# Out-projection of a hybrid decoder trunk: six pairs of heads by seven products in place of five, four plain heads in place of six, and the last part by blocks of tokens

## The chip, the cores and the metric

The kernel runs on one core of one Trainium2 chip. The metric is device time in microseconds (us). The core has TensorE (PE: matmuls, with weight loads in a row of their own, PEld), VectorE (DVE), ScalarE (ACT), GpSimd (POOL) and SyncE (SP), which here only issues transfers. Each works through its own list of instructions in order, and waits where one needs a result that another has not finished.

## The reference

One decoder layer on 512 tokens and 16 learned tokens ahead of them, all float32: RMS norm, one input projection, three token mixers on separate heads (6 gated DeltaNet heads, 5 gated linear attention heads, 5 heads of softmax attention with a forgetting gate), each head 128 wide and multiplied by its own SiLU gate, one output projection of the 16 heads, a residual add and a last RMS norm.

```python
def hybrid_layer(x, norm_w, w_in, ..., w_out):
    h = rms_norm(x, norm_w)
    proj = (h @ w_in).astype(f32)
    ...
    o = jnp.concatenate([o_dn, o_gla, o_fox], axis=-1)[:, PAD:].astype(x.dtype)
    return x + o @ w_out            # o: 512 x 2048, w_out: 2048 x 2048

def reference(...):
    ...
    return rms_norm(h, final_norm_w)[:, N_META:]
```

## The kernel before, in words

**Arithmetic.** Every large matmul is made of three: a float32 operand is split into a high part (rounded to the PE's float32r, an ACT cast) and a low part (the rest, a DVE subtraction), and hi·hi, hi·lo and lo·hi are added up in PSUM. A weight tile is 128 x 1024; `split` (L167 the cast, L168 the subtraction) makes the two parts of each. The raw tiles come through two buffers; every third weight of the products takes three buffers from the pool `six` instead, which also holds the attention heads' keys and queries (`fqk`), the loaded head outputs and the residual.

**Stages.** Until about 792 us the input projection and the three mixers run, interleaved, the last of them attention head 4. The output projection follows, on tiles of 128 tokens by 512 columns (`mms`, L1401: one call is three matmuls). It has two ways:

- *Products.* The first `SH` = 10 heads are taken in pairs. With a pair as a 2 x 2 of blocks (head by half of the tokens) and the weights as a 2 x 2 too, seven products of sums take the place of eight, as in Strassen's scheme in Winograd's form. Each product is 12 matmuls of 512 columns per pair. The operands are a11, a12, s2, s1, s3, s4, a22, in this order of products; the sums of heads that they need are DVE rows of 128 x 256 (L627 and L628 the first sums, L1447 and L1478 the differences), and each operand is split in its turn (L1379 cast, L613 subtraction, 128 x 256 each). The sums of weights for the products are made earlier, as small "chores" that move tiles to scratch memory and add them there by transfers.
- *Plain heads.* The other six heads go by ordinary matmuls. An *early part* (PSUM tiles `pa`) does four of them for column banks 0 to 2, ahead of the products. The *last part* (`pt`, `pz`) does the remaining two heads for banks 0 to 2, then bank 3 with all six heads, with the last block of tokens cut in two halves of 256 columns.

**What sets the order.** A scheduler in the build gives each engine one list; the program fixes parts of it by hand: `paced` rows follow each other on ACT and DVE, `high_priority` puts the splits and the early part's adds forward, and attention head 4's matmuls are placed by number among the early ones. Head 4 goes by four blocks of queries: per block scores (`pfa` L1228, `pfd` L1229), their maximum and weights (DVE L1232 and L1234, ACT L1238, DVE L1239 to L1243), transposes (`pfx` L1246, split by ACT L1250 and DVE L1251), and at the end the product with the values (`pfo` L1276 to L1279).

**After a tile.** `add` (L1420, DVE) adds a PSUM tile to the residual, which `begin` (L1395) has loaded; `square` (L1427, ACT) sums squares for the last norm, `weigh` (L1430, GpSimd) multiplies by the norm's weight, and L1604 to L1614 scale and store.

## Time and profile before

| | |
|---|---|
| median of three runs | 972.87 us (972.32 to 974.4) |
| the profiled execution's own time | 972.28 us |
| its span in the profile | 970.6 us |
| granted TensorE clock, mean | 0.997 |
| PE busy | 960.8 us (99%) |
| DVE busy | 673.0 us (69%) |
| ACT busy | 476.4 us (49%) |
| POOL busy | 221.2 us (23%) |

How to read it: a row of a group gives line, engine, operation, tiles (out<-in), shape and count, then busy time in us, the mean of one in ns, and the engine's idle time before with what ended it. A row of the chain of waits gives start, duration and the work that set the end, followed back from the last instruction. A row of stretches gives from:to and length, then for PE, PEld, DVE, ACT and POOL the busy us and instructions, then the granted clock, the share of the 16 transfer engines that is busy, and GB/s. A timeline row gives start, duration, engine, line and tiles; where it stands for several (x5) the duration is that of all. Next to each other on one engine, rows can overlap by their fill: the pitch is the distance of two starts.

### The profile page before, as it was taken

The page shows a single profiled execution, that of the slowest core. Times are in us where ns is not written, and L with a number is a line of the kernel's source. Part 1 is how long each engine was busy: PE and PEld are TensorE (multiplying, and loading weights), DVE is VectorE, ACT ScalarE, POOL GpSimd, SP SyncE. Part 2 cuts the span into 40 slices and gives each one's busy share as a digit, 9 for nine tenths or more (in the row PEclk, how much of TensorE's full clock was granted, in tenths as well). Part 3 has the DMA queues.
Part 4 walks back from the last instruction along what each step waited for, and adds up shares of the span by engine and source line. Part 5 has one row for each costly group of instructions (what it writes and reads, how often), then busy time and mean ns, then how long its engine had stood idle before and what let it go on. Part 6 is the DMA issues. An engine that isn't in the chain of part 4 may idle for free.

```text
span 970.6 us, 18917 instructions
## 1 busy us (share of the span) xinstructions
PE 960.8 (99%) x7301; PEld 885.2 (91%) x7301; DVE 673.0 (69%) x1463; ACT 476.4 (49%) x1046; POOL 221.2 (23%) x243
## 2 busy tenths in 40 slices
PE   9999999999999999999999999999999999999996
PEld 7899999899999878899999989899999998888885
DVE  6467767877658886434685957867867768977664
ACT  7754433345356233334545545555555545644345
POOL 0032322232123225111213223223332120000033
PEclk9999999999999999999999999999999999999998
DMA  9736677988558687734647575688775587366535
GB/s 353 297 135 208 195 195 213 283 230 224 176 151 232 208 237 196 192 106 104 166 129 189 147 195 172 182 227 210 205 207 163 177 288 273 131 209 222 182 126 174
DMA packets 70336, 191.87 MB, mean 198 GB/s; under 512 B 14078, under 2 KB 17326, under 8 KB 69477
## 3 DMA queue, kind: packets, MB, share of 16 engines
q1 hardware_dynamic: 46048, 152.64, 45.4%
q0 software_dynamic: 15104, 31.66, 18.2%
q10 hardware_dynamic: 9092, 6.36, 2.4%
q8 instruction: 57, 0.93, 0.4%
q14 instruction: 35, 0.28, 0.1%
HBM read 179.94 MB, written 60.88 MB: 248 GB/s over the span
## 4 chain that ended last, share of the span: by engine, by line
PE 98%; DVE 1%; issue 0%; DMA 0%; ACT 0%; SPq 0%; DVEq 0%
PE pp L235 49%; PE pp_a L560 8%; PE pq L1401 6%; PE pp L314 5%; PE pa L1401 3%; PE pt L1401 3%; PE ps L1401 3%; PE pp_c L560 2%; PE pp_d L560 2%; PE pp_b L560 2%; PE pr L1401 1%; PE pss L1046 1%; PE pfo L1276 1%; PE pgate L408 1%; PE pfa L1228 1%; PE pg L704 1%
## 5 line engine op out<-in xcount | busy, mean ns | idle before, releaser
L235 PE MATMUL pp<-xh,wlo 128*128 128x264 f32 (+2 forms) x1120 | 270.0, 305 | 0.0
L235 PE MATMUL pp<-xl,whi 128*128 128x264 f32 (+2 forms) x1120 | 269.6, 305 | 0.0
L235 PE MATMUL pp<-xh,whi 128*128 128x264 f32 (+2 forms) x1120 | 269.5, 305 | 0.0
L167 ACT CAST whi<-raw 128x1024 fp32r<-128x1024 f32 x131 | 137.2, 1047 | 179.5 <-PE pp L235 110.1
L168 DVE TENSOR_TENSOR wlo<-raw,whi 128x1024 fp32r<-128x1024 f32 x131 | 160.6, 1226 | 59.5 <-ACT whi L167 50.1
L235 PEld LDWEIGHTS pp<-xh,wlo 128*128 128x128 f32 x1120 | 181.5, 189 | 9.2 <-DVE wlo L168 0.7
L235 PEld LDWEIGHTS pp<-xh,whi 128*128 128x128 f32 x1120 | 181.3, 188 | 8.7 <-issue 0.2
L235 PEld LDWEIGHTS pp<-xl,whi 128*128 128x128 f32 x1120 | 181.6, 189 | 8.2
L367 POOL TENSOR_SCALAR stc<-cv 128x528 f32<-128x528 f32 (+1 forms) x18 | 27.2, 1513 | 132.0 <-DVE cv L602 120.9
L602 DVE SCALAR_TENSOR_TENSOR cv<-pb,cpk,cv 128x528 f32<-128x528 f32 (+1 forms) x54 | 40.9, 757 | 0.8
L1430 POOL TENSOR_TENSOR acc<-acc,fw 128x512 f32<-128x512 f32 x4 | 6.1, 1544 | 138.4 <-DVE wll L168 138.4
L168 DVE TENSOR_TENSOR wlos<-raws,whis 128x1024 fp32r<-128x1024 f32 x20 | 24.3, 1223 | 15.0 <-ACT whis L167 15.0
L167 ACT CAST whis<-raws 128x1024 fp32r<-128x1024 f32 x20 | 20.7, 1050 | 28.2 <-PE ps L1401 9.2
L314 PE MATMUL pp<-xh,wf 128*128 128x512 f32 x128 | 33.1, 398 | 0.3 <-ACT wf L291 0.3
L314 PEld LDWEIGHTS pp<-xh,wf 128*128 128x128 f32 x128 | 24.2, 190 | 6.1 <-ACT wf L291 0.6
L560 PE MATMUL pp_a<-t,whi 128*128 128x264 f32 (+1 forms) x224 | 29.4, 282 | 0.0
L356 DVE TENSOR_TENSOR pb<-pp,rstd 128x264 f32<-128x264 f32 (+1 forms) x36 | 13.8, 425 | 22.1 <-PE pp L235 22.0
L560 PE MATMUL pp_a<-xl,whi 128*128 128x264 f32 x112 | 28.4, 288 | 0.0
L560 PE MATMUL pp_a<-xh,whi 128*128 128x264 f32 x112 | 28.1, 285 | 0.0
L560 PEld LDWEIGHTS pp_a<-t,whi 128*128 128x128 f32 x224 | 27.6, 188 | 0.0
L474 POOL DMA_DIRECT2D tw<-tw x16 | 13.4, 837 | 60.9 <-DVE wlo L168 29.5
L1401 PE MATMUL pq<-whia,a 128*128 128x512 f32 x80 | 25.5, 394 | 0.0
(487 smaller groups left out, 2058.2 us busy)
## 6 DMA issues: line engine op xcount, KB each, us to landing
raw<-in_w_in SPq DMA_DIRECT2D x103, 512.0 KB, 3.9
ti<-in_w_in SPq DMA_DIRECT2D x28, 512.0 KB, 5.4
raw<-ti SPq DMA_DIRECT2D x28, 512.0 KB, 3.4
tw<-in_w_dn SPq DMA_DIRECT2D x20, 512.0 KB, 5.3
raws<-tw SPq DMA_DIRECT2D x15, 512.0 KB, 3.7
ti<-in_w_in POOLq DMA_DIRECT2D x14, 512.0 KB, 7.0
ti<-ti POOLq DMA_DIRECT2D x14, 512.0 KB, 6.7
tw<-in_w_dn POOLq DMA_DIRECT2D x10, 512.0 KB, 6.7
```

The source lines that it names most:

```text
L167: pace[0] = A.copy(hi, raw).ins
L168: pace[1] = V.tensor_tensor(out=lo, in0=raw, in1=hi.bitcast(F32), op=ALU.subtract).ins
L235: mm = PE.matmul(p_[:, :nt], wt[:, j * m : (j + 1) * m], xx[k][:, t0 : t0 + nt], start=(k == 0 and wt is hi and xx is xh), stop=(k == KT - ...
L314: PE.matmul(begun[i][0][0][:, :S], wt[:, i * P : (i + 1) * P], xx[k][:, NM:T], start=k + n == 0, stop=k == KT - 1 and n == 2)
L356: V.tensor_tensor(out=o, in0=p_[rows], in1=rstd[rows, t0 : t0 + n], op=ALU.mult)
L367: maxes.append(G.tensor_scalar_max(t, src, LOW).ins)
L408: PE.matmul(pgate[a][:, :HT], wg[k // 8][:, k % 8, :], xx[k][:, a * HT : (a + 1) * HT], start=(k == 0 and xx is xh), stop=(k == KT - 1 and ...
L474: x = G.dma_start(out=out_[s], in_=in_[s], accum_op=ALU.add, max_dma_last_dim=2048)
L560: m = PE.matmul(p_[:, cols], wt[:, j * P : (j + 1) * P], xx[j][part_][:, cols], start=first and i == 0, stop=i == len(todo) - 1, skip_grou ...
L602: V.scalar_tensor_tensor(out=c, in0=pb[:, t0 + w : w + T], scalar=cwc[:, blk, w : w + 1], in1=c, op0=ALU.mult, op1=ALU.add)
L704: PE.matmul(pg[:r, j * r : (j + 1) * r], kT[:, j, ts], kT[:, j, ts], start=True, stop=True)
L1401: mm = PE.matmul(p_, o_[:, s], w_, start=(first and n == 0), stop=(last and n == 2), skip_group_check=True)
```

## The change

Four edits.

1. `SH` is 12: six pairs go by products, four heads stay plain. Of these, two are in the early part, so it has one weight of 1024 columns per bank in place of two, and 72 matmuls in place of 144; the products have 504 in place of 420.
2. The operand steps that stood between the early part's six weights now follow its three: all head loads (`load_zr`) go out ahead of the early part, the sums and operands behind each bank.
3. The first sums (two per pair, twelve) are GpSimd's (`G.tensor_tensor`), and are not paced.
4. The last part: two banks in place of three are done for all tokens; bank 2 is done together with bank 3, block of tokens by block, with its add, square and product by the norm's weight in between. Bank 3 has four plain heads in place of six. The chores have a sixth pair of sums of weights.

Behind line 149 the new program's numbers are one higher, from line 610 on one lower: the split is L168 and L169, `mms` L1400, the add L1419, the operand's subtraction L612, the first sums L626 and L627, the differences L1450 and L1476, the attention rows L1227 to L1278.

```diff
-SH = 10
+SH = 12
...
-            paced(V.tensor_tensor(out=r["s1"], in0=r["a22"], in1=r["a21"], op=ALU.subtract),
-                  V.tensor_tensor(out=r["s3"], in0=r["a11"], in1=r["a21"], op=ALU.subtract))
+            G.tensor_tensor(out=r["s1"], in0=r["a22"], in1=r["a21"], op=ALU.subtract)
+            G.tensor_tensor(out=r["s3"], in0=r["a11"], in1=r["a21"], op=ALU.subtract)
...
-    AHEAD = {(0, -1): (0.55, (-1, -2, -3, -4, -5, -6, -7), (0, 1, 2, 3, 4)), ("f", 1): (0.26,)}
+    AHEAD = {(0, -1): (0.55, (-1, -2, -3, -4, -5, -6, -7), (0, 1, 2, 3, 4, 5)), ("f", 1): (0.26,)}
...
-    EARLY, LAST = NP - 2, NP - 6
+    EARLY = NP - 2
...
+    def columns(cc, a, b):
+        src = w_out[cc, a // 2][:, a % 2 * 512 : a % 2 * 512 + (b - a) * 512]
+        return halves(load_half(src, f"o{cc}_{a}"))
+
+    def run(pa, cc, a, b, first, last):
+        w = columns(cc, a, b)
+        for i in range(a, b):
             for tb in range(4):
-                mms(pa[tb], oparts[2 * kp + j], w[j], slice(tb * P, (tb + 1) * P), first and j == 0, last and j == 1)
+                mms(pa[tb], oparts[i], w[i - a], slice(tb * P, (tb + 1) * P), first and i == a, last and i == b - 1)
...
-    steps = [lambda a=a: rest(a, min(a + 2, EARLY)) for a in range(2, EARLY, 2)] + [load_zr]
-    steps += [quarters, lambda: operand("a11"), lambda: operand("a12")]
-    rest(0, 2)
+    steps = [quarters, lambda: operand("a11"), lambda: operand("a12")]
+    rest(0, EARLY)
+    load_zr()
     head["pa", 0] = len(order)
     for cc in range(3):
         pa = banks(psb, f"pa{cc}")
-        for kp in range(EARLY // 2):
-            run(pa, cc, kp, kp == 0, kp == EARLY // 2 - 1)
-            if kp == 1:
-                for tb in range(4):
-                    begin(tb, cc)
-            if steps:
-                steps.pop(0)()
+        run(pa, cc, 0, EARLY, True, True)
+        for tb in range(4):
+            begin(tb, cc)
+        steps.pop(0)()
         with tc.high_priority(offset=1000000):
             for tb in range(4):
                 last = add(tb, cc, pa[tb])
-    for f in steps:
-        f()
     pace[1] = last.ins
     first_sums()
     differences()
...
+    for cc in range(2):
+        pa = banks(psb if cc else psm, f"pt{cc}")
+        run(pa, cc, EARLY, NP, True, True)
+        load_last(cc)
...
+    w2 = columns(2, EARLY, NP)
+    pa, pc = banks(psm, "pt3"), banks(psb, "pt2")
     scaled = []
     for tb in range(4):
         cuts = 2 if tb == 3 else 1
+        for i in range(EARLY, NP):
+            mms(pc[tb], oparts[i], w2[i - EARLY], slice(tb * P, (tb + 1) * P), i == EARLY, i == NP - 1)
+        x = add(tb, 2, pc[tb]).ins
...
+        square(tb, 2)
+        weigh(tb, 2)
```

How it moves instructions, at three places. First DVE before, from the end of attention head 4's block 3 (`fp_9752`, weights of the block) to the second product split; `pa_9990` to `pa_9993` are the early part's last tiles, `wloa` is the low part of a product's weight:

```order
L1243 TENSOR_SCALAR fp_9752<-fp_9752,fsm_9753 128x512
L1241 SCALAR_TENSOR_TENSOR fm_9664<-fp_9752,fsm_9753,fm_9664 128x16
L168 TENSOR_TENSOR wloa_10199<-rawa_10196,whia_10198 128x1024
L1420 TENSOR_TENSOR accs_9969<-accs_9969,pa_9990 128x512
L1420 TENSOR_TENSOR accs_9969<-accs_9969,pa_9991 128x512
L1420 TENSOR_TENSOR accs_10071<-accs_10071,pa_9992 128x512
L1251 TENSOR_TENSOR fplo_9666<-pfx_9762,fphi_9665 128x3x128
L1420 TENSOR_TENSOR accs_10071<-accs_10071,pa_9993 128x512
...
L168 TENSOR_TENSOR wloa_10217<-rawa_10214,whia_10216 128x1024
```

And DVE now, from the adds of the early part's last two tiles to the first product split:

```order
L1419 TENSOR_TENSOR accs_9973<-accs_9973,pa_9939 128x512
L1419 TENSOR_TENSOR accs_9973<-accs_9973,pa_9940 128x512
L1450 SCALAR_TENSOR_TENSOR zr_9811<-zr_9811 128x256
...
L1450 SCALAR_TENSOR_TENSOR zr_9826<-zr_9826 128x256
L1250 TENSOR_TENSOR fplo_9675<-pfx_9710,fphi_9674 128x2x128
L1476 SCALAR_TENSOR_TENSOR zr_9811<-zr_9811 128x256
L1171 TENSOR_TENSOR vlo_9723<-pvf_9717,vhi_9722 128x384
L1231 ISA fp_9741,fsm_9742<-pfa_9737,fqk_9064 128x272
...
L1176 TENSOR_TENSOR fm_9673<-pwf_9727,fm_9673 128x128
L1476 SCALAR_TENSOR_TENSOR zr_9814<-zr_9814 128x256
L612 TENSOR_TENSOR s_0_10016<-zr_9811,s_0_10016 128x256
...
L169 TENSOR_TENSOR wloa_10138<-rawa_10135,whia_10137 128x1024
```

Of the rows left out, the first four are L1450; the others, behind `s_0`, are L1476 and L612 by turns (two more L612) with L1476 last. The first product split now stands behind all adds of the early part, behind the differences of all pairs and behind the first half of operand s2; before, it stood ahead of the last bank's adds.

PE before, where head 4's block 3 has its scores (`pfa_9748`, `pfd_9749`); 34 early matmuls follow there up to the transposes `pfx_9762`:

```order
L1246 MATMUL pfx_9742<-ident,fp_9732 128x128 x3
L1228 MATMUL pfa_9748<-fqk_9059 128x400
L1229 MATMUL pfd_9749<-fqk_9059 128x128
L1401 MATMUL pa_9990<-whio_1_10041,oh_9836 128x512
L1401 MATMUL pa_9991<-whio_1_10041,oh_9836 128x512
```

PE now, from the last early matmul over the scores of block 2 to the first matmul that reads the first product's low part:

```order
L1400 MATMUL pa_9940<-whio_0_9943,ol_9808 128x512
L1245 MATMUL pfx_9710<-ident,fp_9700 128x128 x2
L1168 MATMUL pvf_9717<-ident,vf_9066 128x128 x4
L1174 MATMUL pwf_9727<-ident,fs_9715 128x128
L1227 MATMUL pfa_9737<-fqk_9064 128x272
L1228 MATMUL pfd_9738<-fqk_9064 128x128
L1400 MATMUL pq_10127<-whia_10137,a_0_9915 128x512
...
L1400 MATMUL pq_10130<-whia_10137,a_0_9915 128x512
L1400 MATMUL pq_10127<-wloa_10138,a_0_9915 128x512
```

And from the second product weight's last matmul over block 3 to the use of its weights:

```order
L1400 MATMUL pq_10130<-whia_10155,a_1_9918 128x512
L1245 MATMUL pfx_9751<-ident,fp_9741 128x128 x3
L1227 MATMUL pfa_9757<-fqk_9064 128x400
L1228 MATMUL pfd_9758<-fqk_9064 128x128
L1400 MATMUL pq_10127<-whia_10173,a_2_9921 128x512
...
L1400 MATMUL pq_10130<-whia_10173,a_2_9921 128x512
L1245 MATMUL pfx_9771<-ident,fp_9761 128x128 x4
L1267 MATMUL pfw_9781<-ident,fm_9673 128x128
L1275 MATMUL pfo_9787<-fphi_9674,vhi_9722 128x512
...
L1278 MATMUL pfo_9787<-ptm_9779,fm_9673 128x512 x2
L1400 MATMUL pq_10127<-wloa_10174,a_2_9921 128x512
```

The rows left out are four-tile runs of the same weight and more `pfo`. Blocks 2 and 3 of head 4 now stand behind the early part, among the first three weights of the first product.

More of the change, by code (lines that the diff above doesn't have):

```diff
@@ L151, in load_half @@
         lo = wp.tile([P, 1024], F32R, tag="lo", name=f"wlo{name}")
+        raw, hi, lo = (t[:, : src.shape[-1]] for t in (raw, hi, lo))
         split(raw, hi, lo)
@@ L1402, in mms @@
             order.append(mm.ins)
-    halves = lambda w: [[t[:, j * 512 : (j + 1) * 512] for t in w] for j in range(2)]
+    halves = lambda w: [[t[:, j * 512 : (j + 1) * 512] for t in w] for j in range(w[0].shape[-1] // 512)]
     def load_last(kp):
@@ L1430, in weigh @@
         return G.tensor_tensor(out=acc[tb, cc], in0=acc[tb, cc], in1=fw[cc], op=ALU.mult)
-    def run(pa, cc, kp, first, last):
-        w = halves(load_half(w_out[cc, kp], f"o{cc}_{kp}"))
-        for j in range(2):
+    def columns(cc, a, b):
[4 more added lines that the diff above has]
+        for i in range(a, b):
             for tb in range(4):
-                mms(pa[tb], oparts[2 * kp + j], w[j], slice(tb * P, (tb + 1) * P), first and j == 0, last and j == 1)
+                mms(pa[tb], oparts[i], w[i - a], slice(tb * P, (tb + 1) * P), first and i == a, last and i == b - 1)
     def banks(where, name):
@@ L1553, in tile_hybrid_trunk @@
         fw.append(f)
-    for cc in range(4):
-        pa = banks(psb if cc % 2 else psm, f"pt{cc}")
-        kps = [(NP // 2 - 1,)] * 3 + [range(NP // 2)] * (3 - 3) + [range(LAST // 2)]
-        kps = kps[cc]
-        for kp in kps:
-            run(pa, cc, kp, kp == kps[0], kp == kps[-1])
-            if cc < 3 and (3 == 3 or cc == 2 and kp >= NP // 2 - 3):
-                load_last(kp if cc == 2 and 3 < 3 else NP // 2 - 3 + cc)
-                marks.append(splits[-1])
-        if cc == 3:
-            break
+    for cc in range(2):
+        pa = banks(psb if cc else psm, f"pt{cc}")
+        run(pa, cc, EARLY, NP, True, True)
+        load_last(cc)
+        marks.append(splits[-1])
         for tb in range(4):
```

25 lines of the change are left out of this document (12 added, 13 removed).

## The prediction, on record before the result was known

> **What bounds the kernel now.** I read the page's busy times and chain first, then a table of stretches, then the chain of waits from 792 us on, where the edited code runs.
>
> ```profile
> span 970.6 us, 18917 instructions
> PE 960.8 (99%) x7301; PEld 885.2 (91%) x7301; DVE 673.0 (69%) x1463; ACT 476.4 (49%) x1046; POOL 221.2 (23%) x243
> PE 98%; DVE 1%; issue 0%; DMA 0%; ACT 0%; SPq 0%; DVEq 0%
> ...
> 792.00:829.00 37.00, 36.96 (x172) 29.93 (x172) 27.12 (x71) 15.50 (x34) 4.36 (x4) 1.00 0.80 283
> 829.00:860.00 31.00, 31.00 (x140) 25.39 (x139) 29.81 (x56) 18.77 (x34) 0.00 (x0) 1.00 0.46 158
> 960.00:971.00 11.00, 2.63 (x23) 2.42 (x21) 4.23 (x13) 3.88 (x10) 0.00 (x0) 0.73 0.71 247
> ```
>
> PE is the bound: 98% of the chain, and full in the stretches that the change rewrites. So any matmul taken away is worth its pitch, and any microsecond in which PE waits is a microsecond of the program. The second thing to see is how near VectorE (DVE, third pair of numbers) comes: 27.1 of 37 us while the early part and fox head 4 run, then 29.8 of 31. The early part now is a cover: while PE works it off, the other engines do fox head 4's softmax and prepare the products.
>
> ```profile
> 804.06 0.22 PE pfx L1246 x2
> 804.28 0.44 PE pvf L1169 x4
> 804.72 0.11 PE pwf L1175
> 804.83 0.46 PE pfa L1228 x2
> ...
> 819.99 0.67 PE pfa L1228 x2
> 820.66 0.22 PE pfd L1229 x2
> 820.88 7.85 PE pa L1401 x34
> 828.74 0.44 PE pfx L1246 x4
> 829.17 0.11 PE pfw L1268
> 829.28 0.47 PE pa L1401 x2
> 829.75 2.08 PE pq L1401 x9
> 831.83 1.58 PE pfo L1276 x9
> 901.49 13.93 PE ps L1401 x60
> 960.50 2.14 PE pz L1401 x18
> ```
>
> Each step of fox head 4 has 20 to 34 early matmuls ahead of the next: 34 (7.85 us) between the scores of block 3 (pfd) and the transposes of its weights (pfx), 11 (2.55 us) between those and their use (pfo). A matmul of 512 columns costs 13.93 / 60 = 0.232 us, one of 256 costs 2.14 / 18 = 0.119.
>
> **The change part by part.** *Matmuls.* Before: early part 144, products 7 x 5 pairs x 12 = 420, last part 144 in whole ones (72 for three banks, and 72 for the last bank, in which 36 halves count for 18). After: early 72, products 7 x 6 x 12 = 504, last 48 + 72 = 120. That is 708 against 696: 12 x 0.232 = **-2.8 us**. It is all that the change can gain on PE.
>
> *The first wait.* The early part halves to 16.7 us (72 x 0.232) plus some 2 us of fox matmuls among it, but DVE's work that must be done by then grows. The order on DVE shows it: the last two adds of the early part (pa_9939, pa_9940) stand ahead of six L1450, six L1476 and three L612 rows, fox rows, and only then the split wloa_10138 (L169) that the fifth product matmul reads. An add needs its bank of PE, so none of the rows behind can run before the early part has ended at T.
>
> ```profile
> 807.05 0.43 DVE L1232 CUSTOM_DVE_ANT_0 fp<-pfa,fqk 128x272 f32<-128x272 f32 x1
> 810.22 0.55 DVE L1172 TENSOR_TENSOR vlo<-pvf,vhi 128x384 fp32r<-128x384 f32 x1
> 810.69 0.28 DVE L1177 TENSOR_TENSOR fm<-pwf,fm 128x128 fp32r<-128x128 f32 x1
> 820.54 0.56 DVE L1251 TENSOR_TENSOR fplo<-pfx,fphi 128x384 fp32r<-128x384 f32 x1 [1.06 <-ACT fphi L1250]
> 821.01 0.56 DVE L1232 CUSTOM_DVE_ANT_0 fp<-pfa,fqk 128x400 f32<-128x400 f32 x1
> 821.73 0.35 DVE L1234 CUSTOM_DVE_ANT_0 fp<-pfd,fqk,fsm 128x128 f32<-128x128 f32 x1
> 823.52 0.48 DVE L1243 TENSOR_SCALAR fp<-fp,fsm 128x512 f32<-128x512 f32 x1
> 830.79 1.76 DVE L627 TENSOR_TENSOR zr<-zr 128x256 f32<-128x256 f32 x5
> 832.47 0.42 DVE L628 TENSOR_TENSOR zr<-zr 128x256 f32<-128x256 f32 x1
> 832.80 1.22 DVE L168 TENSOR_TENSOR wloa<-rawa,whia 128x1024 fp32r<-128x1024 f32 x1
> 833.94 0.76 DVE L628 TENSOR_TENSOR zr<-zr 128x256 f32<-128x256 f32 x2
> 850.61 0.68 DVE L1420 TENSOR_TENSOR acc<-acc,pq 128x512 f32<-128x512 f32 x1
> 851.20 0.68 DVE L1420 TENSOR_TENSOR accs<-accs,pq 128x512 f32<-128x512 f32 x1
> ```
>
> These rows give the pitches on a full DVE, from start to start: a 256-wide row (832.47 - 830.79) / 5 = 0.336 us, a split 833.94 - 832.80 = 1.14, an add 851.20 - 850.61 = 0.59. From T: one add 0.6, 15 x 0.336 = 5.0, the fox rows fplo, vlo, L1231 and fm by 0.3 + 0.5 + 0.35 + 0.2 = 1.35, the split 1.2: 8.2 us. PE has in that time the fox matmuls pfx, pvf, pwf, pfa, pfd (0.22 + 0.44 + 0.11 + 0.46, and some 0.1) and four product matmuls (0.93): 2.2 us. It then waits **+6.0 us**. No earlier lead of DVE lowers this, since the adds hold it.
>
> *The second wait.* The ninth row behind is the next split wloa_10156: nine rows (3.0), L1233 (0.3) and 1.14, 4.5 us of DVE against 12 matmuls, 2.8 us: **+1.7**.
>
> *The third weight.* PE then has eight matmuls (1.9 us); DVE, in which the block's ACT step is hidden by a split, needs as long until the transposes of block 2. Then PE does pfx, pfa, pfd and comes to four matmuls on whia_10173, whose buffer is one that fox head 4's keys and queries held: its cast waits for L1233 of block 3, the last reader. On DVE, from pfa: L1231 0.49, a split 1.14, fplo 0.47, L1233 0.28 (each from its start to the next one's), then the cast:
>
> ```profile
> 822.31 0.74 ACT L1238 ACTIVATE fp<-fp,fsm 128x528 f32<-128x528 f32 x1 [1.81 <-DVE fsm L1237]
> 824.17 1.05 ACT L167 CAST whia<-rawa 128x1024 fp32r<-128x1024 f32 x1 [1.03 <-issue]
> 829.21 0.48 ACT L1250 CAST fphi<-pfx 128x384 fp32r<-128x384 f32 x1 [3.99 <-PE pfx L1246]
> ```
>
> 0.49 + 1.14 + 0.47 + 0.28 + 1.05 = 3.4, with signals 3.8, against pfd's 0.22: **+3.6**.
>
> *Fox block 3.* Four matmuls (0.9 us) now stand between that and the transposes, where 34 stood, and none before pfo. The exponential (0.74) waits in ACT's queue behind the cast; with the steps to the end of L1242 it ends some 1.7 us after the cast, so PE waits 0.8; and pfo needs fphi (0.48) and fplo (0.47) behind pfx, with pfw's 0.11 and one pfo matmul for cover, 0.9: **+1.7**. What comes after is the steady run of products, whose DVE rows per weight (a split and one 256-wide row, 1.5 us) are below PE's 2.8: nothing.
>
> *Is DVE on time at T?* Ahead of the last add it has, from the first early split's end, two more splits (2.3), 11 adds (6.5), 12 operand rows (4.0), L372 (0.6) and some 20 fox rows (4), 17.4 us, with waits for two exponentials (2 to 3) against PE's 18.7: even, or 3 late. I take **+1.5** (0 to 3).
>
> *Sums on GpSimd.* A 256-wide sum isn't in the trace on this engine. It lies between half of a 512-wide product and a whole one:
>
> ```profile
> L1430 POOL TENSOR_TENSOR accs<-accs,fw 128x512 f32<-128x512 f32 x8 | 10.1, 1294 | 0.0
> ...
> 789.74 2.23 POOL L1195 TENSOR_TENSOR vf<-vf,rstd 128x528 f32<-128x528 f32 x1 [21.01 <-DVE vf L588]
> 790.71 2.41 DVE L613 TENSOR_TENSOR ol<-zp,oh 128x512 fp32r<-128x512 f32 x2
> ```
>
> I take 0.7: 12 x 0.7 = 8.4 us. DVE is rid of 12 x 0.336 = 4.0 (not in my sums above). But the last two rows show a price: while GpSimd's product ran (789.74 to 791.97), two DVE subtractions took 2.41 us where two of their width at the add's pitch would take 1.3. So DVE lost 1.1 us in the 1.26 they shared, and the product took 2.23 where the eight of L1430 took 1.29. Adds from PSUM beside them show no such growth (0.68). Of DVE's time before T about 8.5 of 19 us is rows with two SBUF operands, so of 8.4 us some 45% meets one: **+3.7** (0, if DVE's waits take it up, to 7.5).
>
> The Trainium skill (GPSIMD Engine Reference, section 1) says that GpSimd shares its SBUF interfaces with VectorE, with contention for instructions with two SBUF inputs; the trace agrees with its 2.41 for 1.3 us. By that rule alone all 8.4 us could be lost to DVE, which is the upper end above, and speaks against this edit.
>
> *Loads.* Twelve head loads, sixteen of the accumulators and three weights now go out in one run ahead of the first product weight; before, they were spread between six weights.
>
> ```profile
> 795.00:800.00 5.00, 5.00 (x24) 4.05 (x23) 1.96 (x8) 0.55 (x3) 3.26 (x4) 1.00 1.06 396
> ```
>
> At 396 GB/s the transfer engines are full. A head or an accumulator is 128x512 f32, 0.26 MB, a weight twice that: 12 x 0.26 + 16 x 0.26 + 2 x 0.52 = 8.4 MB need 21 us there, from about 788 (where the first early cast runs) to 809 or, at a lower rate, 813; T is at about 811. The first product weight lands by T or some us after. I take **+2.5** (0 to 6); the two extra copies of weights to scratch go out much earlier, where PE has cover.
>
> *The end.* Each last block still has 18 matmuls on its bank (4.2 us) as cover for one more add, square and product; the last block's is done 1 us before PE ends. **+0.5** (0 to 2).
>
> Sum: -2.8 + 6.0 + 1.7 + 3.6 + 1.7 + 1.5 + 3.7 + 2.5 + 0.5 = +18.4. The profiled execution took 972.28 us (span 970.6 and 1.7 around it), 0.6 below the median of the runs, so I lay it on either: **991 us**, 1.9% slower.
>
> **Rivals.**
> 1. *It does what the count says*: 972.3 - 2.8 = 969.5, faster. DVE was free for 10 of 37 us, and GpSimd takes work from it. The place is the fifth product matmul: if the split it reads were done by T + 2.2, nothing of the sum but the -2.8 would stand. Against it: the rows behind the last adds cost 8.2 us whatever came before; it turns at their taking 2.2 + 2.8 = 5.0. 4%. Half of the stalls hidden by something I don't see would still leave slower; about even (within 0.2%, what a measurement of this kernel can tell) gets 3%.
> 2. *Only the order stalls*: GpSimd's sums fall into DVE's waits, loads are in time. -2.8 + 13.0 + 0.5 = +10.7: 983. For it: GpSimd has 4.4 us of work in 37, so it may run its sums early. 24%.
> 3. *A slower clock on top.* In the last row of the stretches the granted clock falls to a mean of 0.73 when PE is idle for 8 of 11 us: if it fell to half, that was 0.54 x 11 = 5.9 us of it, from about 965, 2.4 us after PE's last matmul. Stalls of 6 us here are longer than that. What PE runs at half clock for the next 3 us loses 1.5; three stalls, partly hidden as DVE is the bound there, 2 to 5; with the upper ends of port and loads: 991 + 3 + 3.8 + 3.5 = 1001. 16%.
>
> The Trainium skill (TensorE: Matmul & The Clock Gate, Part 1) puts the window at about 3.4 us, free-running, and the clock at half after an idle one. By that the first stall alone would trip it; the trace's 2.4 us fits a window that began earlier.
>
> **How the numbers follow.** Forecast 53% (own range 985 to 998), rival 1 4%, even 3%, rival 2 24%, rival 3 16%. The range runs from 979, where two of the smaller waits of rival 2 fail to appear, to 1003. Faster 0.04, same 0.03, slower 0.93.
>
> **What would show it.** Before about 790 us all as it was. Then: PE idle 6 to 12 us right behind the early part, ended by DVE's wloa (L169), and 3 to 4 us ended by ACT's whia or DVE's L1233 a few us later; DVE near full from 795 to 830; GpSimd's L626 and L627 at 0.7 us or more, and DVE rows beside them above 0.42; PE full from about 850 on; its clock below 1.00 only in the stretch of the stalls. If DVE is idle when PE waits, the loads are the cause. If PE shows no idle time behind the early part, the prediction is wrong in its main term.

## The result, and the profile after

The changed kernel takes 1001.01 us (median of five runs, 999.82 to 1004.08), the kernel before 972.61 (972.32 to 974.4). The ratio is 1.0299, with a 95% interval of 1.0286 to 1.0312: slower by 28.4 us. The range (979 to 1003) held it near its upper end. The forecast of 991 was 10 us too low, outside the 985 to 998 that it called its own, and the time is that of the third rival (1001), though not for all of its reasons.

The profiled execution took 1000.58 us, 1.7 of them around the span. First the page of the changed kernel: span, busy times, and the shares of the chain of waits.

```profile
span 998.9 us, 18949 instructions
PE 969.5 (97%) x7283; PEld 889.2 (89%) x7283; DVE 681.0 (68%) x1462; ACT 479.6 (48%) x1053; POOL 237.3 (24%) x263
PE 78%; DMA 8%; DVE 6%; ACT 3%; issue 2%; POOL 1%; ACTq 0%; SPq 0%; DVEq 0%; POOLq 0%
```

PE is busy 8.7 us longer, with 18 instructions fewer: they ran slower. The span is 28.3 us longer, so PE is also idle for 19.6 us more. The table of stretches shows where, in the order PE, PEld, DVE, ACT, POOL, granted clock, transfer share, GB/s:

```profile
790.00:811.00 21.00, 17.99 (x94) 15.07 (x93) 15.08 (x27) 9.44 (x22) 13.69 (x16) 0.92 1.03 354
811.00:832.00 21.00, 12.21 (x45) 9.01 (x44) 19.25 (x53) 7.36 (x20) 1.20 (x2) 0.82 0.42 156
832.00:855.00 23.00, 18.52 (x62) 14.03 (x61) 12.44 (x28) 8.62 (x17) 0.00 (x0) 0.72 0.37 121
862.00:961.00 99.00, 99.00 (x430) 80.34 (x429) 64.41 (x81) 41.10 (x52) 0.00 (x0) 1.00 0.56 196
```

Before, these stretches had a full PE and a clock of 1.00. Now PE is idle for 3.0 + 8.8 + 4.5 = 16.3 us in 65, and the clock is down to 0.72. From 862 us on PE is full again. PE's rows at the waits, each with its idle time ahead and what ended it, between the first matmul of the early part and the first of the last part:

```profile
794.58 0.94 PE L1400 MATMUL pa<-whio,oh 128*128 128x512 f32 x3
803.99 1.58 PE L1400 MATMUL pa<-whio,oh 128*128 128x512 f32 x3 [3.01 <-ACT whio L168]
814.55 0.77 PE L1400 MATMUL pa<-whio,oh 128*128 128x512 f32 x1 [3.13 <-DVE accs L1419]
824.97 0.49 PE L1228 MATMUL pfd<-fqk 128*128 128x128 f32 x2 [1.90 <-DVE fplo L1250]
830.14 0.79 PE L1400 MATMUL pq<-wloa,a 128*128 128x512 f32 x1 [3.76 <-DVE wloa L169]
831.16 0.63 PE L1400 MATMUL pq<-wloa,a 128*128 128x512 f32 x1
831.59 0.63 PE L1400 MATMUL pq<-whia,a 128*128 128x512 f32 x1
842.61 2.08 PE L1400 MATMUL pq<-whia,a 128*128 128x512 f32 x4 [4.12 <-ACT whia L168]
961.43 1.08 PE L1400 MATMUL pt<-whio,oh 128*128 128x512 f32 x4
```

Two matmuls behind the wait of 3.76 start at 831.16 and 831.59, 0.43 us apart; 512 columns took 0.232 before. The same two ends of the edited part in the kernel before:

```profile
792.13 0.94 PE L1401 MATMUL pa<-whio,oh 128*128 128x512 f32 x3
929.09 0.84 PE L1401 MATMUL pt<-whio,oh 128*128 128x512 f32 x3
```

That gives an account. Early part and products take 961.43 - 794.58 = 166.85 us, before 929.09 - 792.13 = 136.96: 29.9 more. Their matmuls are 84 more in the products and 72 fewer in the early part, 12 x 0.232 = 2.8. The waits are 16.3. The remaining 10.8 is put down to PE at half clock: added up in slices of a quarter of a microsecond, PE's busy time times what the granted clock lacks of 1.00 gives 10.1 of it, and 0.7 stays without a row. What lies on both sides: the early part begins 2.45 us later, and from `pt` to the end is 4.0 shorter, where 24 matmuls fewer should have saved 5.6.

| part of the 28.3 us | us |
|---|---|
| matmuls (12 more, then 24 fewer) | -2.8 |
| early part begins later | +2.45 |
| PE waits, 794 to 861 us | +16.3 |
| PE at half clock (10.1 by the clock's rows) | +10.8 |
| last part saves less than its matmuls | +1.6 |

### The profile page after: what moved, and what is told of

It reads as the page before. It is cut to its first block, busy times and chain, and to the rows that moved or that the text cites. A ratio compares the mean times of both kernels' runs of the same rounds, so it can differ in the third digit from the quotient of the medians.

```text
span 998.9 us, 18949 instructions
## 1 busy us (share of the span) xinstructions
PE 969.5 (97%) x7283; PEld 889.2 (89%) x7283; DVE 681.0 (68%) x1462; ACT 479.6 (48%) x1053; POOL 237.3 (24%) x263
## 4 chain that ended last, share of the span: by engine, by line
PE 78%; DMA 8%; DVE 6%; ACT 3%; issue 2%; POOL 1%; ACTq 0%; SPq 0%; DVEq 0%; POOLq 0%
PE pp L236 38%; PE pq L1400 7%; PE pp_a L561 6%; PE pp L315 5%; PE ps L1400 3%; PE pr L1400 2%; PE pt L1400 2%; DVE wlo L169 2%; PE pp_c L561 1%; PE pp_b L561 1%; PE pp_d L561 1%; DMA zr<-zd 1%; DMA gvt<-zd 1%; DMA raw<-ti 1%; PE pss L1045 1%
## 5 line engine op out<-in xcount | busy, mean ns | idle before, releaser
L168 ACT CAST whi<-raw 128x1024 fp32r<-128x1024 f32 x131 | 137.2, 1047 | 186.7 <-PE pp L236 113.3
L169 DVE TENSOR_TENSOR wlo<-raw,whi 128x1024 fp32r<-128x1024 f32 x131 | 160.9, 1228 | 63.2 <-ACT whi L168 52.3
L169 DVE TENSOR_TENSOR wlos<-raws,whis 128x1024 fp32r<-128x1024 f32 x24 | 28.9, 1223 | 22.9 <-ACT whis L168 22.9
L475 POOL DMA_DIRECT2D tw<-tw x24 | 20.0, 835 | 92.7 <-DVE wlo L169 41.5
L168 ACT CAST whis<-raws 128x1024 fp32r<-128x1024 f32 x24 | 24.4, 1048 | 34.8 <-PE pq L1400 18.1
L1400 PE MATMUL pq<-whia,a 128*128 128x512 f32 x96 | 33.2, 424 | 4.1 <-ACT whia L168 4.1
L168 ACT CAST whia<-rawa 128x1024 fp32r<-128x1024 f32 x18 | 18.6, 1048 | 30.8 <-PE pq L1400 13.8
L169 DVE TENSOR_TENSOR wloa<-rawa,whia 128x1024 fp32r<-128x1024 f32 x18 | 21.9, 1223 | 15.8 <-ACT whia L168 13.1
L1400 PE MATMUL ps<-whis,s 128*128 128x512 f32 x96 | 30.4, 394 | 0.0
L1400 PE MATMUL pq<-whis,s 128*128 128x512 f32 x96 | 30.3, 394 | 0.0
```

The lines of the kernel that those rows point to most:

```text
L168: pace[0] = A.copy(hi, raw).ins
L169: pace[1] = V.tensor_tensor(out=lo, in0=raw, in1=hi.bitcast(F32), op=ALU.subtract).ins
L475: x = G.dma_start(out=out_[s], in_=in_[s], accum_op=ALU.add, max_dma_last_dim=2048)
L1400: mm = PE.matmul(p_, o_[:, s], w_, start=(first and n == 0), stop=(last and n == 2), skip_group_check=True)
```

## The experiments

Medians are of four runs or more, compared with the kernel before on the same chip (972.0 to 972.1). Line numbers of an edited kernel can be one or two off those of the changed one.

### Is the early part a cover? Half of it left out of the kernel before

```diff
-            run(pa, cc, kp, kp == 0, kp == EARLY // 2 - 1)
+            if kp == 0:
+                run(pa, cc, kp, True, True)
+            else:
+                load_half(w_out[cc, kp], f"o{cc}_{kp}")
```

> The kernel before (five pairs), with the matmuls of the third and fourth early head left out: 72 of the 144 early matmuls, 16.7 us of PE. Their weights are still loaded and split, so the other engines do the same. The output lacks these two heads in three banks of columns. Theory 'cover' (with half the early part VectorE and the loads can't keep pace, whatever the number of pairs): waits of 8 to 14 us and a half clock of some us behind them, so of the 16.7 us only 0 to 6 come back: 966 to 972. Rival 'it is the new order of rows, not the cover': waits below 3 us, 955 to 959.

968.79 us, ratio 0.9966 (0.9953 to 0.9979). PE has 72 x 0.232 = 16.7 us less to do, and the kernel gains 3.3. Two of its new waits:

```profile
801.40 0.61 PE L1246 MATMUL pfx<-ident,fp 128*128 128x128 f32 x2 [2.84 <-DVE fm L1241]
823.00 2.08 PE L1401 MATMUL pq<-whia,a 128*128 128x512 f32 x4 [3.59 <-ACT whia L167]
```

With waits of 0.71 and 0.88 they make 8.0 us; 16.7 - 3.3 - 8.0 = 5.4 is left, of which PE's busy time at the lower clock gives 4.5 by its rows. So half of the time that the matmuls took was needed by others, and a good quarter more went to the clock behind the waits. The two waits differ: the one of 2.84 ends with VectorE's weights of an attention block, the one of 3.59 with the cast of the first product's weight, ahead of which the chain has that weight's own transfer (6.40 us from 815.43). The early part covers loads as well as other engines. No other edit of the change is in this kernel, so this much comes with the smaller early part by itself.

### Who makes the sums: VectorE in place of GpSimd

```diff
-            G.tensor_tensor(out=r["s1"], in0=r["a22"], in1=r["a21"], op=ALU.subtract)
-            G.tensor_tensor(out=r["s3"], in0=r["a11"], in1=r["a21"], op=ALU.subtract)
+            paced(V.tensor_tensor(out=r["s1"], in0=r["a22"], in1=r["a21"], op=ALU.subtract),
+                  V.tensor_tensor(out=r["s3"], in0=r["a11"], in1=r["a21"], op=ALU.subtract))
```

> The twelve first sums go back to VectorE, behind the early part's last add; nothing else changes. Theory 'order' (the waits come from what stands behind the early part's last adds on VectorE): twelve more rows of 0.336 us stand between the last add and the first product split, so the first wait grows by 4.0 us and the time is 1003 to 1006. Rival 'shared port' (GpSimd's sums slow VectorE before the early part ends, my +3.7): the early rows shrink back to their pitch, the waits of 3.0 and 3.1 us inside the early part shrink by 3 us or more together, and the time is 995 to 999.

1001.03 us, ratio 1.0295 (1.0275 to 1.0316): no change against the changed kernel, which neither theory gave. First the changed kernel's GpSimd rows, alone and beside VectorE, and two of VectorE's operand rows beside such sums:

```profile
795.48 0.74 POOL L626 TENSOR_TENSOR zr<-zr 128x256 f32<-128x256 f32 x1 [7.20 <-DMA zr<-zd]
808.85 1.72 POOL L626 TENSOR_TENSOR zr<-zr 128x256 f32<-128x256 f32 x1
806.69 1.60 DVE L612 TENSOR_TENSOR a<-zr,a 128x256 fp32r<-128x256 f32 x2
```

Then VectorE's and PE's rows in the edited kernel:

```profile
808.22 0.76 DVE L612 TENSOR_TENSOR a<-zr,a 128x256 fp32r<-128x256 f32 x2
820.14 2.10 DVE L626 TENSOR_TENSOR zr<-zr 128x256 f32<-128x256 f32 x6
839.20 0.88 PE L1245 MATMUL pfx<-ident,fp 128*128 128x128 f32 x3 [5.55 <-DVE fm L1240]
```

Both theories are half right. Without GpSimd beside it two operand rows take 0.76 us in place of 1.60, the wait of 3.13 in the early part is gone, and from its first matmul to the products' it takes 25.1 us in place of 30.6. Part of that is the clock behind the wait. So the sums on GpSimd do cost VectorE time there. But the twelve sums now stand on VectorE behind the early part's end, and PE pays 5.55 us for them at attention block 2. The edit of the sums is worth nothing either way: VectorE's rows follow each other without a gap on both sides of that end, from 805.9 to 819.0 and from 819.5 to 839 us in this kernel.

### Is it the place of the work? Sums and operands after the first product

Sums, differences and the operands from s2 on are issued behind the first of the seven products, not ahead of it.

```diff
-    first_sums()
-    differences()
-    operand("s2")
-    operand("s1")
...
-    operand("s3")
-    operand("s4")
-    operand("a22")
...
+    first_sums()
+    differences()
+    operand("s2")
...
+    operand("a22")
```

> The first sums, the differences and the operands s2, s1, s3, s4, a22 are issued behind the first product, not ahead of it; the work is the same. On VectorE only one add and attention rows then stand between the early part's end and the first product split. Theory 'order': PE's waits for that split (1.9 and 3.8 us) fall below 1 us together, with the half clock behind them; the wait for the third weight (4.1) stays; 992 to 995. If GpSimd's sums also slowed VectorE before the early part's end, the waits of 3.0 and 3.1 us shrink too: 988 to 991. Rival 'the loads are late, not VectorE': waits of the same sum with another releaser, 999 to 1002.

995.29 us, ratio 1.0252 (1.0224 to 1.028), 5.7 below the changed kernel and just above the 992 to 995 that were expected. PE's rows:

```profile
805.85 1.65 PE L1400 MATMUL pa<-whio,oh 128*128 128x512 f32 x3 [3.00 <-ACT whio L168]
816.48 0.47 PE L1400 MATMUL pa<-whio,oh 128*128 128x512 f32 x1 [2.06 <-DVE accs L1419]
824.56 1.20 PE L1400 MATMUL pq<-whia,a 128*128 128x512 f32 x4 [0.71 <-ACT whia L168]
826.24 0.50 PE L1400 MATMUL pq<-wloa,a 128*128 128x512 f32 x1 [0.48 <-DVE wloa L169]
```

The wait at the first product weight, 1.90 + 3.76 in the changed kernel, is 0.71 + 0.48. So it was the sums and differences between the early part's last add and the split. The two waits inside the early part stay, 3.00 and 2.06 (3.13 before): they have another cause. One thing was not expected: the wait for the third weight, 4.12 in the changed kernel, is 2.08 here.

### Is that cause the loads? The early weights ahead of the head loads

Two steps. First the one before with the sums of weights spread a little faster, so that they end at 721 us:

```diff
-    AHEAD = {(0, -1): (0.55, ...
+    AHEAD = {(0, -1): (0.61, ...
```

> The kernel of the later sums (995.3 us) with the rate of the sums of weights at 0.61 in place of 0.55 per weight, so that the sixth pair's are done by about 731 us, as the five pairs' were before, and not by 787. Theory 'upstream': attention head 3's steps are no longer late, the early part begins at 792.4 to 793.5: 991 to 993. Rival 'the transfers only wait elsewhere': stalls of 2 to 4 us earlier in the program, 994 to 997.

993.47 us, ratio 1.0216 (1.0194 to 1.0237), 1.8 below the kernel with only the sums later, which is within the spread of the two (989.91 to 994.63, and 993.76 to 999.68). The start of the early part, 794.35 us in the profile, did not come back to the 792.4 to 793.5 that were expected. Then also the early part's second weight ahead of the head loads:

```diff
-    load_zr()
...
+    ws = [columns(0, 0, EARLY)]
...
+        if cc < 2:
+            ws.append(columns(cc + 1, 0, EARLY))
+        if cc == 0:
+            load_zr()
```

> As the kernel before it in this list, with the second early weight's transfer issued ahead of the twelve head loads. Theory 'loads': the wait of 3.0 us for the second early weight and the half clock behind it (1.3) go, while VectorE's operand rows, which wait for the heads, come later: the wait for the early part's adds grows from 2.1 to 4 or 5. Net -1.5 to -3.5 against that kernel: 988 to 991. Rival 'the same bytes, the same wait': all of it comes back at the adds, 991 to 994.

990.51 us, ratio 1.0194 (1.0179 to 1.0209). The medians differ by the 3.0 us that were expected, but the two intervals overlap, and the profiled executions (989.91 and 990.77) stand the other way round: a gain by this step isn't shown. Nor does it show the cause of the wait for `whio`: that wait is absent already from the profile of the first step, the fastest of its four runs. What remains are the rows. In the changed kernel ACT's cast of that weight waits 6.84 us for its transfer, which goes out at 796.7 us, behind six heads and four blocks of the residual; in the two steps it goes out at 793.2 and 792.0. In the second step it still stands behind six of the twelve heads in the queue: what it overtook is the residual. The second wait of the changed kernel, 3.13, has these two steps of the chain right ahead of it (start, duration):

```profile
801.26 6.80 DMA zr<-zd
808.07 4.55 DMA accs<-in_xtok
```

What is left in both steps is a wait that ends with VectorE's rows, here PE's row in the first and the last transfer in the chain of the second, where the wait is 3.79:

```profile
811.06 0.47 PE L1400 MATMUL pa<-whio,oh 128*128 128x512 f32 x1 [3.73 <-DVE fsm L1236]
806.54 4.83 DMA accs<-in_xtok
```

That transfer brings the residual for an add of the early part and lands at 811.37; the add starts at 811.41, with VectorE full since 799 us. Before it VectorE's operand rows run beside GpSimd's sums, three in 2.48 us where one and two alone take 0.42 and 0.76. So VectorE and the residual's loads end this wait together, and no run parts them.

### The clock: filling the last wait with matmuls that do nothing

Attention head 4's `pfd` of block 3 is done 18 times in place of once, ahead of the wait of 4.12 us. It is waste, but PE's clock should stay up.

```diff
-            PE.matmul(pd[:, :P], qT[:, ts], kT[:, ts], start=True, stop=True)
+            for _ in range(18 if (h, b) == (FOX_HEADS - 1, 3) else 1):
+                PE.matmul(pd[:, :P], qT[:, ts], kT[:, ts], start=True, stop=True)
```

> The score matmul of attention head 4's block 3 on the diagonal is done 18 times in place of once, so PE works some 2 us longer into its wait of 4.1 us for the third product weight's cast; what is computed stays the same. Theory 'clock': an idle time of 2 us doesn't lower the clock, so the matmuls from the end of that wait on (9 us at half the clock) run at full, -3 to -5 us, 996 to 998. Rival 'the idle time before it had set the clock, or the waits of several us add up': the clock row of that stretch stays at 0.5 to 0.66, time 1001 (1000 to 1002).

1002.84 us, ratio 1.0315 (1.0299 to 1.033): the total missed, it is no faster. The stretch itself did what was expected. First the changed kernel, then the edited one:

```profile
845.00:850.00 5.00, 4.64 (x16) 3.76 (x15) 1.21 (x2) 1.66 (x6) 0.00 (x0) 0.50 0.00 0
```

```profile
841.82 4.18 PE L1229 MATMUL pfd<-fqk 128*128 128x128 f32 x36
847.53 1.21 PE L1401 MATMUL pq<-whia,a 128*128 128x512 f32 x4 [1.53 <-ACT whia L168]
847.00:852.00 5.00, 3.45 (x15) 2.31 (x16) 1.49 (x5) 2.87 (x9) 0.00 (x0) 1.00 0.00 1
```

The idle time is 1.53 in place of 4.12, the clock 1.00 in place of 0.50, and from the wait's end to the first `pt` it takes 116.5 us in place of 118.8 (both worked out from the starts), although new waits of 0.47, 0.46 and 0.50 stand behind it. So this wait cost its length and then, by the clock's rows, some 4.5 us more that PE lost to the clock behind it. Where the gain of 2.3 went: in this execution the early part began at 798.09 and its add wait was 4.3 us. Why it began 3.5 us later than in the changed kernel, with an edit that stands behind it, isn't settled: PE is idle for 2.0 us between 200 and 400 us and for 3.7 between 700 and 792, where the changed kernel's profile has 0.5 and 1.2. The profiles of kernels with twelve heads by products begin it anywhere from 793.8 to 798.1, but for the last one below.

### What moved the start: only the sums of weights, in the kernel before

The kernel before, with a sixth pair's sums of weights made and not used.

```diff
-    AHEAD = {(0, -1): (0.55, (-1, -2, -3, -4, -5, -6, -7), (0, 1, 2, 3, 4)), ...
+    AHEAD = {(0, -1): (0.55, (-1, -2, -3, -4, -5, -6, -7), (0, 1, 2, 3, 4, 5)), ...
```

> The kernel before (five pairs) with the sums of weights of a sixth pair made as well and not used: eight more accumulating transfers in halves and four more copies of weight tiles, all else as before. Theory 'upstream' (these sums are why the early part begins at 793.8 to 798.1 us in the profiles of the new kernels and at 792.4 before): the early part begins at 794 to 797 and the time is 974 to 977. Rival 'something else moved it': early part at 792.4, time 972 (971.5 to 973).

978.85 us, ratio 1.0079 (1.0054 to 1.0105), against 974 to 977 expected. The sixth pair alone, without a single product, costs 6.8 us; the prediction had it at nothing. First a chain step and rows of this kernel, then the cast and the stretch of the kernel before:

```profile
757.54 7.46 DMA raw<-in_w_in
765.10 1.04 ACT L167 CAST whi<-raw 128x1024 fp32r<-128x1024 f32 x1 [6.08 <-DMA raw<-in_w_in]
766.93 0.49 PE L1229 MATMUL pfd<-fqk 128*128 128x128 f32 x2 [2.50 <-DVE fplo L1251]
796.86 0.94 PE L1401 MATMUL pa<-whio,oh 128*128 128x512 f32 x3
```

```profile
760.52 1.05 ACT L167 CAST whi<-raw 128x1024 fp32r<-128x1024 f32 x1 [2.00 <-PE pvf L1169]
755.00:760.00 5.00, 5.00 (x44) 5.00 (x43) 4.04 (x8) 3.52 (x7) 0.00 (x0) 1.00 0.45 152
```

The additions of weights are transfers that accumulate in scratch memory, issued by GpSimd. Before, the last goes out at 731 us, with a sixth pair at 789. Beside them a load of a 128 x 1024 weight takes 7.46 us, where the five such loads between 735 and 785 us in the kernel before have a median of 3.5 (all 103 of the program 3.9, here 4.1); the transfer engines are busy for 0.79 and 0.86 of the two stretches of 5 us in which it runs. The cast behind it stands in ACT's queue for 6.08 us, the split and the attention's rows behind the cast, and PE waits 2.50. The early part begins 4.7 us later; PE is idle for 3.3 us between 700 and 792 in all, and the rest stands in smaller pieces ahead of that. What the prediction had called covered was not: the additions go out early enough, but they run beside weights that are due. That it is the additions and not the four copies of weights made with them is read from this place, where only additions are new; no run has one without the other.

### The last part in its old shape

Three banks for all tokens, then the last, as before, with twelve heads by products.

```diff
-    for cc in range(2):
+    for cc in range(3):
...
-        for i in range(EARLY, NP):
-            mms(pc[tb], oparts[i], w2[i - EARLY], ...)
-        x = add(tb, 2, pc[tb]).ins
...
-        square(tb, 2)
-        weigh(tb, 2)
```

> Only the last part goes back to the old shape: banks 0 to 2 for all tokens, then bank 3 by blocks (four plain heads, as now). The profile after shows PE's last matmul at 989.4 and the last add only at 991.4, with VectorE and ScalarE taking turns for 14 us before. Theory 'the tail became VectorE's': -2.0 us, 999.0 (998 to 1000). Rival 'the output stores set the end': no change, 1001 (within 0.7).

1001.01 us, ratio 1.0294 (1.0278 to 1.0311): no change, as the rival had it. In both profiles it takes 37.5 us from the first `pt` to the end. So the blocks of tokens cost next to nothing. What the last part loses stands behind PE's last matmul (989.13), where VectorE is late in the changed kernel:

```profile
989.13 0.28 PE L1400 MATMUL pz<-wlh,ol 128*128 128x256 f32 x1
989.25 1.21 DVE L1614 TENSOR_SCALAR accs<-accs,frs 128x512 f32<-128x512 f32 x1 [0.34 <-ACT frs L1605]
990.38 0.74 DVE L1611 SCALAR_TENSOR_TENSOR accs<-accs,frs,fw 128x512 f32<-128x512 f32 x1
991.29 0.41 DVE L1419 TENSOR_TENSOR accs<-accs,pz 128x256 f32<-128x256 f32 x1
```

Before, the last add starts 0.3 us after PE's last matmul; here 2.2 us, behind two rows that scale blocks already done. In the old shape it starts 0.4 us after it, but the same two scalings then stand between the add and the sum of squares. From PE's last matmul to the last row of ScalarE it takes 3.1 us before, 4.9 now and 4.3 in the old shape; the stores behind that take 5.1, 4.8 and 5.6. So what the old shape wins on the engines the stores take back, as the rival said, and both shapes lose about the same. With four plain heads in bank 3 in place of six, a block in the old shape gives PE 12 matmuls, 2.8 us, in place of 4.2: that the fewer heads are the cause is argued from this, and no run with only that changed was made.

### A version with three early heads

Sums later, sums of weights faster, and three early heads in place of two (108 matmuls, one head late). Attention head 3's output is kept on the chip for it.

```diff
-    EARLY = NP - 2
+    EARLY = NP - 1
...
-        run(pa, cc, 0, EARLY, True, True)
+        run(pa, cc, 0, 2, True, False)
+        run(pa, cc, 2, EARLY, False, True)
```

> As the kernel of the sooner sums of weights, with three plain heads in the early part in place of two (108 matmuls, 25 us) and one in the last part; head 3's output stays in SBUF for it. Theory 'cover' (the waits come from the early part's halving): PE's waits behind 790 fall from some 10 us to 5 or less and the clock stays at 1.00; the last part's blocks then have 15 matmuls (3.5 us) against the 4.3 us that VectorE and ScalarE take per block, +2 to +3 at the end: 977 to 982. Rival 'order alone, whatever the cover': 986 to 991.

984.51 us, ratio 1.0133 (1.0118 to 1.0148); it missed 977 to 982, but gives back 16.5 of the 28.4 us. The longest wait inside the early part is this one, and the clock there is 1.00:

```profile
806.93 0.50 PE L1402 MATMUL pa<-wloo,oh 128*128 128x512 f32 x1 [0.91 <-DVE wloo L169]
```

Between the early part's first matmul and the last part's PE is idle for 4.0 us, against 9.8 in the kernel with two early heads and the same faster sums of weights, so the cover does what was expected of it; the load of head 3 that falls away may have a share in that. What it lost on the expectation is 4 us ahead of the early part (796.50 against 792.13) and the end: from PE's last matmul (969.80) to the end it takes 12.9 us, 4.7 more than before where 2 to 3 were expected. There GpSimd's products and VectorE's scaling run side by side, and a scaling takes 1.80 us that alone takes 0.74:

```profile
961.86 7.77 POOL L1431 TENSOR_TENSOR accs<-accs,fw 128x512 f32<-128x512 f32 x6
968.37 1.80 DVE L1613 SCALAR_TENSOR_TENSOR accs<-accs,frs,fw 128x512 f32<-128x512 f32 x1
970.49 0.74 DVE L1613 SCALAR_TENSOR_TENSOR accs<-accs,frs,fw 128x512 f32<-128x512 f32 x1
```

Last, the same with the sixth pair's sums of weights made during the first two products, where PE is full in the kernel before, and the first five pairs' as before:

```diff
-    AHEAD = {(0, -1): (0.61, ..., (0, 1, 2, 3, 4, 5)), ...
+    AHEAD = {(0, -1): (0.55, ..., (0, 1, 2, 3, 4)), ...
...
+    jobs(out_jobs(5))
+    rate[0], due[0] = 0.5, -2
```

> The kernel with three early heads (984.5 us), but five pairs' sums of weights at the old rate of 0.55, and the sixth pair's made while the first two products run, where they are needed only at the end of the third. Theory 'upstream': attention head 3 is as before, the early part begins at 792 to 793 (796.5 there), 980 to 981.5. Rival 'the transfers cost wherever they are': the products' weights come late instead, waits in the first two products, 983 to 986.

981.5 us, ratio 1.0093 (1.0076 to 1.011), as expected. The early part begins where it did before:

```profile
792.40 0.85 PE L1402 MATMUL pa<-whio,oh 128*128 128x512 f32 x3
```

This is the fastest version with twelve heads by products, and its median is still 9.4 us above that of the kernel before. By the profiles it is 9.7: -2.8 is matmuls, 0.3 the later start, 4.6 PE's waits from there to the last part, 5.2 what lies behind PE's last matmul; 2.4 I could not place.

## Why the prediction was right or wrong

**Direction and main mechanism: right.** The early part is a cover, and halving it costs more than 12 matmuls bring. The kernel before with half of it left out shows this without any other edit, and three early heads in place of two bring most of the waits back down. What the prediction said first, that any matmul taken away is worth its pitch, does not hold here: 72 of them, 16.7 us, gave 3.3.

**The first wait: right.** Predicted 8.2 us from the early part's last add to the split, and 6.0 of PE's waiting. The rows:

```profile
821.88 0.69 DVE L1419 TENSOR_TENSOR accs<-accs,pa 128x512 f32<-128x512 f32 x1 [0.71 <-PE pa L1400]
822.49 2.09 DVE L1450 SCALAR_TENSOR_TENSOR zr<-zr 128x256 f32<-128x256 f32 x6
828.87 1.21 DVE L169 TENSOR_TENSOR wloa<-rawa,whia 128x1024 fp32r<-128x1024 f32 x1
```

821.88 to 828.87 + 1.21 is 8.2 us; PE waited 1.90 + 3.76 = 5.7. The forecast had one wait; the attention's `pfd` took a part of it. With the rows moved away 4.5 of it went, which confirms the cause.

**The third weight: right in size**, 4.12 for 3.6, its path only in part. It ends with the cast of `whia`, as predicted. The forecast had that cast wait for L1233 of block 3, the last reader of the buffer. The rows:

```profile
840.51 0.34 DVE L1233 CUSTOM_DVE_ANT_0 fp<-pfd,fqk,fsm 128x128 f32<-128x128 f32 x1
840.99 0.62 ACT L1368 CAST oh<-zp 128x512 fp32r<-128x512 f32 x1 [1.74 <-DMA zp<-zd]
841.51 1.04 ACT L168 CAST whia<-rawa 128x1024 fp32r<-128x1024 f32 x1
```

L1233 is done by 840.85, and the chain does not run through it: ahead of the cast stands that of a plain head, whose load has just landed, and its 0.5 us are about what 4.12 has above 3.6. In the run that filled this wait with matmuls the cast does wait for VectorE's row of block 3. So the predicted path is as long as forecast, and another of nearly the same length stood beside it.

**The second wait and attention block 3: too high**, 1.7 each, measured 0 and 0.35. PE ran at half clock there, so the same matmuls gave the other engines twice the time. For block 3 the run that filled the wait bears this out: at full clock its waits there are 0.47, 0.46 and 0.50, together near the forecast. For the second wait it is an argument only. A term worked out at full clock and the clock's own term are not to be added.

**VectorE late at the early part's end, sums on GpSimd, loads: about right in sum, wrong in place.** Predicted 1.5 + 3.7 + 2.5 = 7.7 us; measured were two waits inside the early part, 3.01 for a weight behind the head loads and 3.13 that ends with VectorE's adds, 6.1 together. Ahead of the second the chain has the residual's load, landed at 812.62 for an add at 813.74, so by the rows the loads have a part in it; yet with the sums on VectorE it is gone. I had looked for the loads' cost at the first product weight; it fell on the early part's own second weight. The 0.7 us for a sum on GpSimd was 0.74 alone, and the price to VectorE was real (0.76 to 1.60 for two rows). Undoing the edit does not give it back, as the run shows. The prediction's 8.4 us for the case that all is lost is not the upper end of its own range, which is 7.5. The rule of the Trainium skill that spoke against the edit (GPSIMD Engine Reference, section 1, shared interfaces) agrees with these rows, and they add that GpSimd pays too: 0.74 us becomes 1.72.

**The clock: the step that failed most.** The forecast's sum had nothing for it; only the third rival had, with +3. It was 10.8 us. Behind each of the waits of 3.0 us or more PE ran at half clock for 3.1 to 9.0 us (some of the 10.8 is a remainder; the clock's rows give 10.1). The mistake was in the working of that rival: I took the fall at the program's end, seen 2.4 us after the last matmul, allowed one stretch of 1.5 us lost for each of three stalls, and called VectorE the bound behind them. There were four stalls, two of them in the early part, and behind the last one the half clock held for 9 us (842.6 to 851.65). By the Trainium skill (TensorE: Matmul & The Clock Gate, Part 1) one idle window of about 3.4 us halves the clock and about as long at work restores it. The stretches of 3.5 and 3.1 us behind the first two waits agree; the waits of 2.84 and 3.0 us that already lowered it are shorter than that page's window, and so are two of 2.08 us in other kernels here; the 4.7 and 9.0 us at half clock behind the last two waits are longer.

**"The two extra copies of weights to scratch go out much earlier, where PE has cover": wrong.** With the sums made from them they alone cost the kernel before 6.8 us. In the changed kernel's profile the early part begins 2.45 us late, and "before about 790 us all as it was" fell with it. The price, where the run shows it, lay in the slowed load of another weight. The kernel before could have warned of it: its loads of `raw` take a median of 4.1 us between 640 and 735 us, where such additions run, and 3.2 and 3.5 (by source) between 735 and 790, where none does. The prediction should have bounded the term from both sides rather than set it at nothing.

**The end: 1.6 for 0.5**, inside the bound given (0 to 2); by the rows two scalings stand in the way at the end, in either shape of the last part.

Together: -2.8 as predicted; waits of PE behind 794 us 16.3 for a predicted 20.7 (18.4 without the matmuls' -2.8 and the end's 0.5); half clock 10.8, start 2.45 and end 1.6 for a predicted 0.5. That the range held the time is thus in part luck: the waits came out 4.4 lower than forecast, which made up for a third of the clock and the start, two terms that the sum had at nothing.

## What to carry to other kernels

Before work is taken off the engine that bounds a kernel, ask what the others do meanwhile: independent matmuls that stand between dependent steps are paid for anyway, and 16.7 us of them left out gave 3.3. Where a stall of 2 us or more is expected on TensorE, look for a slower clock behind it and price that with the stall, here up to two thirds as much again (10.8 for 16.3 us of waits), and expect neighbouring waits on slower engines to shrink in return. Transfers that "go out early" are not free because they are early: look for the next load with a due time and for the queue that stands behind it.

## What the runs showed of the hardware that was not expected

- The length of a wait alone did not decide whether PE's clock fell. It fell with each wait of 2.8 us or more behind 790 us in these profiles, the shortest of 2.82 and 2.84. In the kernel with the sums later it also fell 1.4 us after a wait of 2.08, and in the one with the faster sums of weights as well 1.3 us after the wait below, both times past one more of 0.49. In the kernel with the weights first it did not fall behind the same two waits, nor elsewhere behind waits of 2.11, 2.21 and 2.50. In the changed kernel the wait of 3.76, which follows one of 1.90 and 1.4 us of work, has the clock at half after 1.6 us.

```profile
830.67 1.19 PE L1400 MATMUL pq<-whia,a 128*128 128x512 f32 x4 [2.08 <-ACT whia L168]
```

- Accumulating transfers slowed one ordinary load that ran beside them: 7.46 us in place of a median of 3.5 for 128 x 1024 f32, with the transfer engines busy for 0.79 and 0.86 of that time, where they were for 0.45 before.
- GpSimd and VectorE slow each other in both directions: 0.74 to 1.72 us for a sum on GpSimd, 0.76 to 1.60 for two operand rows and 0.74 to 1.80 for a scaling on VectorE.
